# One part of the input split a chunk sooner, a fourth low part by DMA, and another order of buffers in the last way down

## The chip, the cores and the metric

The kernel is one launch on one core of a Trainium2 chip. The metric is the device time of a launch in microseconds, the median of several runs; lower is better. The core has five engines that each work through a queue of their own in order and meet only at semaphores: TensorE (PE, matmuls and weight loads), VectorE (DVE), ScalarE (ACT), GpSimd (POOL) and SyncE (SP, which here issues nearly all loads). PE accumulates into banks of PSUM, 128 x 512 floats each.

## The reference

A trunk of two layers over 512 tokens of width 1024. Each layer is a half-step SwiGLU FFN, a mixer (mLSTM in layer 0, gMLP in layer 1), a second FFN and a gated per-layer embedding ("ple"), each added to `x` and normalised. The change lies in the FFNs, of which there are four:

```python
def swiglu_ffn(x, w_gu, w_d):                 # x 512 x 1024, w_gu 1024 x 5632, w_d 2816 x 1024
    g, u = jnp.split(x @ w_gu, 2, axis=-1)
    return (jax.nn.silu(g) * u) @ w_d
# in each layer i:
x = layer_norm(ALPHA * x + 0.5 * swiglu_ffn(x, ffn1_wgu[i], ffn1_wd[i]), ...)
x = layer_norm(ALPHA * x + mixer(x), ...)
x = layer_norm(ALPHA * x + 0.5 * swiglu_ffn(x, ffn2_wgu[i], ffn2_wd[i]), ...)
x = layer_norm(ALPHA * x + sigmoid(x @ ple_wg[i] + ple_bg[i]) * (p[i] @ ple_wp[i]), ...)
```

Everything is float32.

## The kernel before

**High and low parts.** A float32 operand is taken apart into a high part in the type float32r (`whi`, `xh`, `fhi`) and what is left, the low part (`wlo`, `xl`, `flo`). A product of two operands is three matmuls, high x high, high x low and low x high: `mm3`, lines 353 to 355. The high part is a copy by ACT. The low part is made in one of two ways, in `Weights.fill`:

```python
self.nc.scalar.activation(hi[:, s], src[:, s], AF.Copy)                       # L242
if make in self.by_dma or low == "dma" and make not in self.in_place:
    self.nc.scalar.activation(lo[:, s], src[:, s], AF.Copy, scale=-1.0)       # L248
    self.nc.gpsimd.dma_start(lo[:, s], src[:, s], accum_op=OP.add)            # L249
elif not self.apart:
    self.nc.vector.tensor_sub(lo[:, s], src[:, s], hi[:, s].bitcast(F32))     # L251
```

So a low is a subtraction on DVE, or a second ACT copy with the sign turned and a DMA issued by POOL that adds the source to it ("by DMA"). With `apart`, DVE's subtraction is put off and issued later by `lows()` (L257).

**An FFN in six chunks.** The 22 blocks of hidden columns go in chunks of 2, 4, 4, 4, 4 and 4 (0 to 5). Of each chunk PE computes the way up (gate and up columns), then SiLU x up gives `h`, and `h` goes the way down. The way down of a chunk runs one chunk later, woven into the next way up, in a 2 x 2 block form with 7 products in place of 8 (`Group`; the sums of its weights are formed on DVE in lines 111 to 117, its operand is split in lines 905 and 908, and line 727 adds the product to `x`). The way down of chunk 5 has no way up behind it: it is the "plain" way down, `dps`, with four weight tiles of 128 x 1024 from two loads.

**The way up of chunks 4 and 5** uses 7 products too, per pair of hidden blocks: four pairs in an FFN, 0 and 1 in chunk 4, 2 and 3 in chunk 5. The weights of a pair are two loads (gate and up, 128 x 2048 each) and come in seven forms, `Weights.up_forms`: a11, a12, s2, s1, s3, s4, a22, the products 0 to 6. a11, a12, s4 and a22 are the loaded quarters or what the sums left there; s2 is formed in place on DVE (lines 141, 142), s3 in lines 149 and 150 once the lows of a12 and s2 are made, and s1 is what line 141 left. `UP_BY_DMA` names the products whose low goes by DMA: a12, s3, s4, a22 so far; the lows of a11, s2 and s1 are DVE's.

The other side of these products are forms of `x`: three quarters of `x`, which exist in `xh` and `xl`, and four sums that `UpForms` makes: t3 = x22 - x12, t2 = t3 + x11, t1 = x22 - t2 and t4 = x21 - t2, each of 128 x 1024 and split in a high and a low. The sums take one step at a time of `self.steps` in chunk 3; what `self.last` holds is done in chunk 4 behind the product with that number. Working buffers `b` and `c` carry t3 and t2, `d` carries t4. `c` has the buffer `f0` that t4's low takes over; `b` has the buffer `wlo` of the pool `late` that t2's low takes over, so that t2's low cannot be made before t3 is split from `b`.

A product's turn in `up_products` sets the order of all that the engines get:

```python
pair.product(r)          # PE: 24 matmuls of 128 x 256
group.add()              # DVE: L727 for the product of the way down before
pair.take(r)             # ACT copies the bank to `us` (L1047) for r = 0, 2, 3; DVE adds (L1050) for 1, 4, 5
group.finish_form(); W.lows()                 # DVE: L908, L257
if c == UP_FROM and s in formed.last:
    formed.last[s]()
W.release(); pair.gate(r)                     # more whi/wlo; ACT: Silu (L1061) for r = 1, 5
```

and behind every second product one of the way down. Line 1066 is the multiplication by SiLU, lines 358 and 359 are `split`, line 1000 is t4's high, line 1004 t2's low (t3's split stands in front of it) and line 1009 t4's low.

**Buffers.** Split weights lie in four buffers of kind `main`, which are filled in the order of use as they come free; the forms of the way down lie in a buffer of kind `rows`, and late in pair 3 a second one, `rowsx`, is opened behind product 2 in place of `UpForms`' tiles of the pool `late`. `add_rows` gives the four tiles of the plain way down a kind each. SP issues a load as soon as a raw buffer is free; no queue is ordered by a planner.

Of the kernel before, what the change touches and what calls it, by code (L numbers as in the profile page):

```python
# [10 lines left out]
F32 = mybir.dt.float32  # L11
F32R = mybir.dt.float32r
AF = mybir.ActivationFunctionType
# [29 lines left out]
W_BUFS = 4  # L43
EXTRA = 2
PLE_EXTRA = 3
UP_BY_DMA = (1, 4, 5, 6)


class Weights:
# [77 lines left out]
    def up_forms(self, g, u):  # L127
# [34 lines left out]
        self.after.update({s2: (a11,), s3: (a12, s2)})  # L162
        self.by_dma.update(made[r][1] for r in UP_BY_DMA)
        return [("main", js, make) for js, make in made]
# [158 lines left out]
def hybrid_trunk(ctx: ExitStack, tc, x, p, ln_g, ln_b, ffn1_wgu, ffn1_wd, ffn2_wgu, ffn2_wd,  # L323
# [25 lines left out]
    vec, sca, pool = nc.vector, nc.scalar, nc.gpsimd  # L349
# [7 lines left out]
    def split(hi, lo, src):  # L357
        sca.activation(hi, src, AF.Copy)
        vec.tensor_sub(lo, src, hi.bitcast(F32))
# [51 lines left out]
    def kp(w):  # L411
        return w.rearrange("(kb p) c -> p kb c", p=P)
# [4 lines left out]
    def add_pairs(w, a0, b0):  # L417

        W.add((w_cols(w, a0), cols2), (w_cols(w, b0), cols2))

    def kinds_of(kind, at):
        return kind if isinstance(kind, str) else kind[at:at + 2]

    def add_rows(w, kb, n, kind="main"):
        for k in range(0, n, 2):
            W.add((kp(w)[:, kb + k:kb + k + 2, :], rows2), kind=kinds_of(kind, k))
# [9 lines left out]
    LAST = len(FFN_CHUNKS) - 1  # L436
# [4 lines left out]
    def ffn_weights(wgu, wd, name, ple=False):  # L441
        starts = [sum(FFN_CHUNKS[:c]) for c in range(LAST + 1)]

        def forms(c):
            m = FFN_CHUNKS[c] // 2

            def quarter(i, j):
                k = starts[c] + m * i
                return kp(wd)[:, k:k + m, j * 512:(j + 1) * 512]
            loads = [W.add_load(quarter(i, j), n, name) for i, j, n in ((0, 0, 2), (0, 1, 1), (1, 1, 1), (1, 0, 2))]  # L450
            return W.forms("rows", *((j, slice(None)) for j in loads))

        first = len(W.order)
        for at in range(starts[UP_FROM]):
            if at == 0 or at == starts[UP_FROM] - 1:
                W.add(*((kp(wgu)[:, :, c0:c0 + P], [slice(None)]) for c0 in (at * P, HID + at * P)))
            elif at % 2:
                add_pairs(wgu, at * P, HID + at * P)
        tiles = W.order[first:]
        del W.order[first:]  # L460
        for c, n in enumerate(FFN_CHUNKS):
            down_w = deque(forms(c - 1) if c else ())
            if c >= UP_FROM:
                products = []
                for b in range(starts[c], starts[c] + n, 2):
                    products += W.up_forms(*(W.add_load(kp(wgu)[:, :, c0:c0 + 2 * P], 2) for c0 in (b * P, HID + b * P)))
                for s, product in enumerate(products):
                    W.order.append(product)
                    if s % 2:
                        W.order.append(down_w.popleft())  # L470
                continue
            for i in range(2 * n):
                W.order.append(tiles[2 * starts[c] + i])
                if down_w:
                    W.order.append(down_w.popleft())
        if ple:
            W.add_hook("rows", lambda hi, lo: turn_p.pop()(hi, lo))
        add_rows(wd, starts[LAST], 4, ["rows", "rowsx", "main", "main"] if ple else ["main", "rows", "rows", "rowsx"])


    ML_SLOTS = (2, 3, 4, 5, 6, 7, 11)
# [71 lines left out]
    def ple_weights(i):  # L553
        add_rows(ple_wp[i], 0, 2)
        add_wide(ple_wg[i], 0, ["extra", "extra", "extra", "main"])
        add_wide(ple_wg[i], 512, ["rows", "rows", "rowsx", "rows2"])

    ffn_weights(ffn1_wgu[0], ffn1_wd[0], (0, 0))
    ml_weights()
    ffn_weights(ffn2_wgu[0], ffn2_wd[0], (0, 2), True)  # L560
    ple_weights(0)
    ffn_weights(ffn1_wgu[1], ffn1_wd[1], (1, 0))
    gm_weights()
    ffn_weights(ffn2_wgu[1], ffn2_wd[1], (1, 2), True)
# [108 lines left out]
    class Norm:  # L673


        def __init__(self, layer, k, out=None):
            self.out, self.st, self.rs = out, {}, {}
            self.deferred = out is None and k != 2
            self.at = (layer * 4 + k) * KB
            gb = act.tile([P, 2, D], F32, name="gb", tag="gb")  # L680
            self.g_bc, self.b_bc = gb[:, 0], gb[:, 1]
            o = (layer * 4 + k) * D
            sca.dma_start(self.g_bc, row_ap(ln_g, o, D))
            sca.dma_start(self.b_bc, row_ap(ln_b, o, D))
# [265 lines left out]
    class UpForms:  # L950


        def __init__(self, pool, late):

            f32 = lambda at, tag: at.tile([P, 4, 256], F32, name="x_" + tag, tag=tag)
            a = [tmp.tile([P, 2, 256], F32, name="x_a", tag="pad", bufs=3) for _ in range(2)]
            b, c = f32(late, "wlo"), f32(pool, "f0")
            both = act.tile([P, 2, 4, 256], F32R, name="t1", tag="gb")
            self.t1, self.t2, self.t4 = [both[:, 0], both[:, 1]], [], []
            self.t3 = self.quarter(0, 1)  # L960
            whole, halves = slice(0, 4), (slice(0, 2), slice(2, 4))

            def joined(dst, k, t, s=whole):
                vec.tensor_add(dst, *(p[:, s].bitcast(F32) for p in self.quarter(k, t)))

            def f32r(to, at, tag):
                to.append(at.tile([P, 4, 256], F32R, name="t_" + tag, tag=tag))
                return to[-1]

            def x22():  # L970
                for i, s in enumerate(halves):
                    joined(a[i], 1, 1, s)

            def t3():
                for i, s in enumerate(halves):
                    vec.tensor_sub(b[:, s], a[i], b[:, s])

            def t1():
                for i, s in enumerate(halves):
                    vec.tensor_sub(a[i], a[i], c[:, s])  # L980

            def split_t1():
                for i, s in enumerate(halves):
                    split(self.t1[0][:, s], self.t1[1][:, s], a[i])

            self.steps = [
                x22, lambda: joined(b, 0, 1), t3, lambda: joined(c, 0, 0), lambda: vec.tensor_add(c, b, c),
                lambda: sca.activation(f32r(self.t2, late, "whi"), c, AF.Copy), t1, split_t1]

            d = [tmp.tile([P, 2, 256], F32, name="x_d", tag="pad", bufs=3) for _ in range(2)]  # L990

            def x21():
                for i, s in enumerate(halves):
                    joined(d[i], 1, 0, s)

            def t4():
                hi = f32r(self.t4, pool, "f1")
                for i, s in enumerate(halves):
                    vec.tensor_sub(d[i], d[i], c[:, s])
                    sca.activation(hi[:, s], d[i], AF.Copy)  # L1000

            def t3_t2():
                split(*self.t3, b)
                vec.tensor_sub(f32r(self.t2, late, "wlo"), c, self.t2[0].bitcast(F32))

            def t4_low():
                lo = f32r(self.t4, pool, "f0")
                for i, s in enumerate(halves):
                    vec.tensor_sub(lo[:, s], d[i], self.t4[0][:, s].bitcast(F32))

            self.steps += [x21, t4]
            self.last = {0: t3_t2, 3: t4_low}
            self.right = [self.quarter(0, 0), self.quarter(1, 0), self.t2, self.t1, self.t3,
                          self.quarter(1, 1), self.t4]

# [894 lines left out]
```

## Time and profile before

| | |
|---|---|
| median of 3 runs | 2246.17 us (2243.39 to 2249.09) |
| the profiled execution | 2251.26 us, its span 2249.5 |
| mean granted TensorE clock in the span | 0.994 |
| packets of DMA | 287.31 MB, of these POOL's queue 58.91 MB |
| copies to `whi` from 128 x 1024 or smaller tiles of `wraw` on ACT (L242) | 388, 1047 ns each |
| matmuls of the way up in 7 products (`ups`, three lines) | 3 x 512, 285 to 288 ns each |

How to read it: a group has its line, engine, operation, tiles and shapes, then busy time and mean length of one, then the idle time of the engine just ahead of these instructions and what ended it. In the lists of single instructions the first number is the start in us from the begin of the span, the second the length (with "x2" and more: of all of them together, gaps included). The granted clock is the share of full speed that TensorE was allowed.

### The profile page before, as it was taken

The page shows a single profiled execution, that of the slowest core. Times are in us where ns is not written, and L with a number is a line of the kernel's source. Part 1 is how long each engine was busy: PE and PEld are TensorE (multiplying, and loading weights), DVE is VectorE, ACT ScalarE, POOL GpSimd, SP SyncE. Part 2 cuts the span into 40 slices and gives each one's busy share as a digit, 9 for nine tenths or more (in the row PEclk, how much of TensorE's full clock was granted, in tenths as well). Part 3 has the DMA queues.
Part 4 walks back from the last instruction along what each step waited for, and adds up shares of the span by engine and source line. Part 5 has one row for each costly group of instructions (what it writes and reads, how often), then busy time and mean ns, then how long its engine had stood idle before and what let it go on. Part 6 is the DMA issues. An engine that isn't in the chain of part 4 may idle for free. (4 is left out here: it accounts for less than half of the span.)

```text
span 2249.5 us, 29438 instructions
## 1 busy us (share of the span) xinstructions
PE 2207.3 (98%) x11669; PEld 1896.6 (84%) x11669; DVE 1693.8 (75%) x2452; ACT 1059.5 (47%) x1492; POOL 159.0 (7%) x199
## 2 busy tenths in 40 slices
PE   9999999999999999999999999999999999999998
PEld 8888987888888888888888888987888888888877
DVE  5668787786776776688786768886788767678887
ACT  4334655464646433356444334655345453336542
POOL 1000110111101100001000000110001100001000
PEclk9999999999999999999999999999999999999999
DMA  6323754456847443246532333754437733335551
GB/s 200 104 93 113 179 137 131 108 143 133 155 123 155 126 131 94 93 121 161 169 122 66 115 101 112 178 135 137 140 76 151 168 122 113 103 113 124 139 168 57
DMA packets 215538, 287.31 MB, mean 128 GB/s; under 512 B 6836, under 2 KB 161588, under 8 KB 215400
## 3 DMA queue, kind: packets, MB, share of 16 engines
q1 hardware_dynamic: 168080, 211.83, 29.2%
q0 software_dynamic: 40704, 58.91, 16.4%
q10 hardware_dynamic: 6616, 14.69, 2.0%
q8 instruction: 92, 1.51, 0.3%
q14 instruction: 46, 0.38, 0.1%
HBM read 224.58 MB, written 2.11 MB: 101 GB/s over the span
## 5 line engine op out<-in xcount | busy, mean ns | idle before, releaser
L242 ACT ACTIVATE whi<-wraw 128x1024 fp32r<-128x1024 f32 (+1 forms) x388 | 400.0, 1047 | 247.8 <-DVE wraw L142 90.8
L353 PE MATMUL fps<-xh,whi 128*128 128x512 f32 x800 | 311.4, 389 | 0.0
L354 PE MATMUL fps<-xl,whi 128*128 128x512 f32 x800 | 311.2, 389 | 0.0
L355 PE MATMUL fps<-xh,wlo 128*128 128x512 f32 x800 | 311.2, 389 | 0.0
L251 DVE TENSOR_TENSOR wlo<-wraw,whi 128x1024 fp32r<-128x1024 f32 (+1 forms) x214 | 257.0, 1216 | 52.5 <-ACT whi L242 51.9
L353 PE MATMUL gps<-whi,fhi 128*128 128x512 f32 x644 | 251.9, 391 | 0.0
L354 PE MATMUL gps<-wlo,fhi 128*128 128x512 f32 x644 | 251.6, 391 | 0.0
L355 PE MATMUL gps<-whi,flo 128*128 128x512 f32 x644 | 251.3, 390 | 0.0
L242 ACT ACTIVATE whi<-wquarter 128x1024 fp32r<-128x1024 f32 (+1 forms) x140 | 135.6, 969 | 201.0 <-PE gps L355 132.8
L249 POOL DMA_DIRECT2D wlo<-wraw x112 | 114.2, 1020 | 1500.5 <-ACT wlo L248 1309.6
L251 DVE TENSOR_TENSOR wlo<-wquarter,whi 128x1024 fp32r<-128x1024 f32 (+1 forms) x92 | 97.6, 1061 | 160.6 <-ACT whi L242 160.6
L727 DVE TENSOR_TENSOR xt<-xt,gps 128x512 f32<-128x512 f32 x302 | 193.0, 680 | 1.2 <-PE gps L355 1.2
L355 PEld LDWEIGHTS fps<-xh,wlo 128*128 128x128 f32 x800 | 150.2, 188 | 31.3
L353 PEld LDWEIGHTS fps<-xh,whi 128*128 128x128 f32 x800 | 150.2, 188 | 31.1
L354 PEld LDWEIGHTS fps<-xl,whi 128*128 128x128 f32 x800 | 150.2, 188 | 30.9
L353 PE MATMUL ups<-xh,whi 128*128 128x256 f32 x512 | 147.6, 288 | 12.2 <-ACT us L1047 12.2
L355 PE MATMUL ups<-xh,wlo 128*128 128x256 f32 x512 | 147.5, 288 | 1.1 <-DMA wlo<-wraw 1.1
L354 PE MATMUL ups<-xl,whi 128*128 128x256 f32 x512 | 146.1, 285 | 0.0
L355 PEld LDWEIGHTS gps<-whi,flo 128*128 128x128 f32 x644 | 120.9, 188 | 26.2
L353 PEld LDWEIGHTS gps<-whi,fhi 128*128 128x128 f32 x644 | 121.1, 188 | 23.9
L354 PEld LDWEIGHTS gps<-wlo,fhi 128*128 128x128 f32 x644 | 121.1, 188 | 23.6
L905 ACT ACTIVATE fhi<-h 128x512 fp32r<-128x512 f32 (+1 forms) x140 | 80.8, 577 | 120.2 <-DVE h L1151 50.4
(361 smaller groups left out, 5056.5 us busy)
## 6 DMA issues: line engine op xcount, KB each, us to landing
wraw<-in_ffn_wgu_dram SPq DMA_DIRECT2D x79, 1024.0 KB, 7.3
wlo<-wraw POOLq DMA_DIRECT2D x112, 512.0 KB, 5.9
wquarter<-in_ffn_wd_dram SPq DMA_DIRECT2D x64, 512.0 KB, 3.8
wraw<-in_ml_w_in_dram SPq DMA_DIRECT2D x24, 1024.0 KB, 5.8
wraw<-in_gm_w_in_dram SPq DMA_DIRECT2D x15, 1024.0 KB, 5.6
wraw<-in_ffn_wgu_dram SPq DMA_DIRECT2D x17, 512.0 KB, 4.9
wraw<-in_ffn_wd_dram SPq DMA_DIRECT2D x8, 1024.0 KB, 6.3
wraw<-in_ml_w_out_dram SPq DMA_DIRECT2D x8, 1024.0 KB, 5.1
```

The lines of the kernel that those rows point to most:

```text
L242: self.nc.scalar.activation(hi[:, s], src[:, s], AF.Copy)
L249: self.nc.gpsimd.dma_start(lo[:, s], src[:, s], accum_op=OP.add)
L251: self.nc.vector.tensor_sub(lo[:, s], src[:, s], hi[:, s].bitcast(F32))
L353: mm(ps, st[0], mv[0], start=start, stop=False, skip_group_check=more)
L354: mm(ps, st[0], mv[1], start=False, stop=False, skip_group_check=more)
L355: mm(ps, st[1], mv[0], start=False, stop=stop, skip_group_check=more)
L727: vec.tensor_add(dst, dst, ps)
L905: sca.activation(hi, src, AF.Copy)
```

## The change

It has three parts, and each applies to all four FFNs.

1. t2 gets its low in chunk 3, behind its high, by `split`; for that `b` moves to the buffer `f1`, which t4's high takes over. t4's high in turn moves from chunk 3 to chunk 4, behind product 3, and t4's low from behind product 3 to behind product 4 of the first pair.
2. s1's low goes by DMA.
3. The four weight tiles of the plain way down take other buffers: where the ple follows (FFNs 1 and 3) `rowsx` and `rows` change places, and in FFNs 0 and 2 `rowsx` holds the third tile and `rows` the second and fourth.

```diff
-UP_BY_DMA = (1, 4, 5, 6)
+UP_BY_DMA = (1, 3, 4, 5, 6)
...
-        add_rows(wd, starts[LAST], 4, ["rows", "rowsx", "main", "main"] if ple else ["main", "rows", "rows", "rowsx"])
+        add_rows(wd, starts[LAST], 4, ["rowsx", "rows", "main", "main"] if ple else ["main", "rows", "rowsx", "rows"])
...
-            b, c = f32(late, "wlo"), f32(pool, "f0")
+            b, c = f32(pool, "f1"), f32(pool, "f0")
...
+            def split_t2():
+                split(f32r(self.t2, late, "whi"), f32r(self.t2, late, "wlo"), c)
+
             self.steps = [
                 x22, lambda: joined(b, 0, 1), t3, lambda: joined(c, 0, 0), lambda: vec.tensor_add(c, b, c),
-                lambda: sca.activation(f32r(self.t2, late, "whi"), c, AF.Copy), t1, split_t1]
+                split_t2, t1, split_t1]
...
             def t4():
+                for i, s in enumerate(halves):
+                    vec.tensor_sub(d[i], d[i], c[:, s])
+
+            def t4_high():
                 hi = f32r(self.t4, pool, "f1")
                 for i, s in enumerate(halves):
-                    vec.tensor_sub(d[i], d[i], c[:, s])
                     sca.activation(hi[:, s], d[i], AF.Copy)
-
-            def t3_t2():
-                split(*self.t3, b)
-                vec.tensor_sub(f32r(self.t2, late, "wlo"), c, self.t2[0].bitcast(F32))
...
-            self.last = {0: t3_t2, 3: t4_low}
+            self.last = {0: lambda: split(*self.t3, b), 3: t4_high, 4: t4_low}
```

SP's order of loads is the same in both; POOL's queue gets four more DMAs in each FFN. From the second hunk on, line numbers are higher by 2 or 3 in the new kernel (L1047 is L1049, L1050 is L1052, L1061 is L1063, L1151 is L1153).

How it moves instructions, at three places. A row is line, operation, output <- inputs and shape, in the order of the engine's queue; "x2" stands for two in a row.

DVE in FFN 0, around the first product of chunk 4, before (`x_f_1300` is the buffer `c`, `x_wlo` the buffer `b`; the row of L1004 is t2's low, the first L251 the low of s1):

```order
L1151 SCALAR_TENSOR_TENSOR h<-sg,fps 128x512
L251 TENSOR_TENSOR wlo<-wraw,whi 128x1024
L251 TENSOR_TENSOR wlo<-wquarter,whi 128x1024
L908 TENSOR_TENSOR flo<-h,fhi 128x512
L359 TENSOR_TENSOR xl<-x_wlo,xh 128x4x256
L1004 TENSOR_TENSOR t_wlo<-x_f_1300,t_whi 128x1024
L149 TENSOR_TENSOR wraw<-wraw 128x1024
L150 TENSOR_TENSOR wraw<-wraw 128x1024
```

and now (`x_f_1299` is the buffer `b`):

```order
L1153 SCALAR_TENSOR_TENSOR h<-sg,fps 128x512
L251 TENSOR_TENSOR wlo<-wquarter,whi 128x1024
L908 TENSOR_TENSOR flo<-h,fhi 128x512
L359 TENSOR_TENSOR xl<-x_f_1299,xh 128x4x256
L149 TENSOR_TENSOR wraw<-wraw 128x1024
L150 TENSOR_TENSOR wraw<-wraw 128x1024
```

Two subtractions fewer stand ahead of L149 and L150. t2's low stands about seventeen rows earlier in this queue, behind the step that makes t2 in chunk 3.

ACT at the same place, before (the row of L1000 is t4's high in two halves, the first L242 the high of s2, the second that of s1, the row of L1047 the copy behind product 0):

```order
L242 ACTIVATE whi<-wraw 128x1024
L1000 ACTIVATE t_f_1710<-x_d 128x512 x2
L905 ACTIVATE fhi<-h 128x512
L242 ACTIVATE whi<-wraw 128x1024
L242 ACTIVATE whi<-wquarter 128x1024
L905 ACTIVATE fhi<-h 128x512
L1047 ACTIVATE us<-ups 128x512
```

and now (the row of L248 is s1's copy with the sign turned, for the DMA):

```order
L242 ACTIVATE whi<-wraw 128x1024
L905 ACTIVATE fhi<-h 128x512
L242 ACTIVATE whi<-wraw 128x1024
L248 ACTIVATE wlo<-wraw 128x1024
L242 ACTIVATE whi<-wquarter 128x1024
L905 ACTIVATE fhi<-h 128x512
L1049 ACTIVATE us<-ups 128x512
```

t4's high is gone from here, and s1's second copy stands two rows further on.

DVE in pair 2 of FFN 0, from the low of s2 to the addition for the gate, before (the second `wlo<-wraw` is s1's low):

```order
L257 TENSOR_TENSOR wlo<-wraw,whi 128x1024
L149 TENSOR_TENSOR wraw<-wraw 128x1024
L150 TENSOR_TENSOR wraw<-wraw 128x1024
L257 TENSOR_TENSOR wlo<-wraw,whi 128x1024
L257 TENSOR_TENSOR wlo<-wquarter,whi 128x1024
L908 TENSOR_TENSOR flo<-h,fhi 128x512
L727 TENSOR_TENSOR xt<-xt,gps 128x512 x2
L111 TENSOR_TENSOR wquarter<-wquarter 128x1024
L112 TENSOR_TENSOR wquarter<-wquarter 128x1024
L1050 TENSOR_TENSOR us<-us,ups 128x512
```

and now:

```order
L257 TENSOR_TENSOR wlo<-wraw,whi 128x1024
L149 TENSOR_TENSOR wraw<-wraw 128x1024
L150 TENSOR_TENSOR wraw<-wraw 128x1024
L257 TENSOR_TENSOR wlo<-wquarter,whi 128x1024
L908 TENSOR_TENSOR flo<-h,fhi 128x512
L727 TENSOR_TENSOR xt<-xt,gps 128x512 x2
L111 TENSOR_TENSOR wquarter<-wquarter 128x1024
L112 TENSOR_TENSOR wquarter<-wquarter 128x1024
L1052 TENSOR_TENSOR us<-us,ups 128x512
```

One subtraction fewer stands between L150 and the addition.

ACT at the end of FFN 0's last pair, before (the rows of L242 here are the highs of the plain way down's tiles and, behind them, of the mixer's weights; `gb` are the layer norm's weights):

```order
L1047 ACTIVATE us<-ups 128x512
L242 ACTIVATE whi<-wraw 128x1024 x2
L683 DMA gb<-in_ln_g_dram 128x1024
L684 DMA gb<-in_ln_b_dram 128x1024
L1061 ACTIVATE us<-us 128x512
L358 ACTIVATE wquarter<-us 128x2x256 x2
L242 ACTIVATE whi<-wraw 128x1024 x5
```

and now:

```order
L1049 ACTIVATE us<-ups 128x512
L242 ACTIVATE whi<-wraw 128x1024 x3
L683 DMA gb<-in_ln_g_dram 128x1024
L684 DMA gb<-in_ln_b_dram 128x1024
L1063 ACTIVATE us<-us 128x512
L358 ACTIVATE wquarter<-us 128x2x256 x2
L242 ACTIVATE whi<-wraw 128x1024 x4
```

The high of the third tile has moved ahead of the two loads and of the Silu in line 1061, now 1063.

## The prediction

> **What bounds the kernel now.** I read the page first, then the waits of PE, then the places of those waits in order of time.
>
> ```profile
> span 2249.5 us, 29438 instructions
> PE 2207.3 (98%) x11669; PEld 1896.6 (84%) x11669; DVE 1693.8 (75%) x2452; ACT 1059.5 (47%) x1492; POOL 159.0 (7%) x199
> ```
>
> PE is busy for 98% of the span and the change leaves its matmuls as they are. So it can only touch the idle 42 us and the matmuls that run at a lower clock. The waits of PE, longest in total first (line waited for: total us, times, longest):
>
> ```profile
> PE ups L353 <- ACT us L1047: 12.2, 12, 2.5
> PE dps L353 <- DVE xt L727: 7.0, 3, 3.5
> PE ups L354 <- DVE t_wlo L1004: 5.1, 4, 1.3
> PE dps L353 <- ACT whi L242: 2.4, 2, 1.2
> PE ups L355 <- DMA wlo<-wraw: 2.2, 3, 1.1
> PE dps L354 <- DVE wlo L257: 1.5, 2, 0.8
> ```
>
> That is 30.4 us. All of it lies in the last two chunks of the four FFNs and the plain way down behind them, which is where the change works. I number the FFNs 0 to 3 and the pairs of an FFN's last two chunks 0 to 3.
>
> **Part one: t2 is split a chunk sooner.** Pair 0 of FFN 0, start and length of each row, idle time before it in brackets:
>
> ```profile
> 222.81 0.38 PE L354 MATMUL ups<-t_wlo,whi 128*128 128x256 f32 x1 [1.29 <-DVE t_wlo L1004]
> 221.53 1.23 DVE L1004 TENSOR_TENSOR t_wlo<-x_f,t_whi 128x1024 fp32r<-128x1024 f32 x1
> 223.92 1.22 DVE L150 TENSOR_TENSOR wraw<-wraw 128x1024 f32<-128x1024 f32 x1
> 213.21 1.24 ACT L1000 ACTIVATE t_f<-x_d 128x512 fp32r<-128x512 f32 x2 [3.10 <-DVE x_d L999]
> 225.18 1.06 ACT L242 ACTIVATE whi<-wraw 128x1024 fp32r<-128x1024 f32 x1 [5.53 <-DVE wraw L150]
> 240.60 0.28 PE L354 MATMUL ups<-t_f,whi 128*128 128x256 f32 x1
> 201.54 1.23 DVE L251 TENSOR_TENSOR wlo<-wquarter,whi 128x1024 fp32r<-128x1024 f32 x1 [2.18 <-ACT whi L242]
> ```
>
> Removed: PE stands still for just the 1.29 us of t2's low; four times, the 5.1 of the waits. Of the 12.2 us for the copies `us`, 7.0 stand in pair 2 (below) and 4.4 in pair 3; the other 0.8, 0.2 in each FFN, stand right behind this wait and hang on L150, which comes earlier, so they go too. Added a chunk sooner: DVE waits for t2's high (one ACT copy, 1.06) and makes the low (1.23). I cost this 2.3 us at nothing, because DVE stood idle for 2.18 us at 201.54; 0.2 us would remain if the cover failed, more only if it were gone.
>
> Moved: t4's high goes from chunk 3 to product 3 and its low behind product 4's lows. DVE has no gap from L150 on except for about 0.5 us twice, where it waits for ACT. Ahead of L150 its queue loses t2's low and s1's low, and the 1.24 us of t4's high no longer stand ahead of the fhi copy that DVE waits for; going through the queue with these durations, L150 starts at about 221 (2.9 sooner) and t4's low has its first half at 239.6. PE, 1.5 us sooner, wants it at 240.60 - 1.5 = 239.1. That is a new wait of 0.5 us, between 0 and 2.0 (if DVE gained only 1.2 us). Four times: +2.0. Part one: -5.1 - 0.8 + 2.0 = **-3.9**.
>
> **Part two: s1's low by DMA.** It moves 16 lows (4 FFNs x 4 pairs) from DVE to ACT and POOL; each costs by these groups:
>
> ```profile
> L248 ACT ACTIVATE wlo<-wraw 128x1024 fp32r<-128x1024 f32 x112 | 116.9, 1044 | 0.0
> L257 DVE TENSOR_TENSOR wlo<-wraw,whi 128x1024 fp32r<-128x1024 f32 x62 | 74.4, 1219 | 6.1 <-ACT whi L242 6.0
> ```
>
> So DVE has 16 x 1.219 = 19.5 us less, ACT 16 x 1.044 = 16.7 us more. What of this reaches PE is decided in pair 2, where the long waits stand (DVE, ACT and PE of FFN 0, then the same PE wait of the other FFNs):
>
> ```profile
> 273.74 1.23 DVE L141 TENSOR_TENSOR wraw<-wraw 128x1024 f32<-128x1024 f32 x1 [6.84 <-DMA wraw<-in_ffn_wgu_dram]
> 284.58 1.22 DVE L257 TENSOR_TENSOR wlo<-wraw,whi 128x1024 fp32r<-128x1024 f32 x1
> 279.11 1.04 ACT L242 ACTIVATE whi<-wraw 128x1024 fp32r<-128x1024 f32 x1
> 284.75 1.06 ACT L242 ACTIVATE whi<-wraw 128x1024 fp32r<-128x1024 f32 x1 [2.65 <-DVE wraw L150]
> 291.75 0.63 ACT L1061 ACTIVATE us<-us 128x512 f32<-128x512 f32 x1 [3.09 <-DVE us L1050]
> 286.27 0.28 PE L353 MATMUL ups<-t,whi 128*128 128x256 f32 x1
> 294.38 0.39 PE L353 MATMUL ups<-xh,whi 128*128 128x256 f32 x1 [2.37 <-ACT us L1047]
> 1059.49 0.38 PE L353 MATMUL ups<-xh,whi 128*128 128x256 f32 x1 [1.62 <-ACT us L1047]
> 1475.16 0.39 PE L353 MATMUL ups<-xh,whi 128*128 128x256 f32 x1 [0.54 <-ACT us L1047]
> 2109.84 0.39 PE L353 MATMUL ups<-xh,whi 128*128 128x256 f32 x1 [2.49 <-ACT us L1047]
> ```
>
> Product 4 waits for the copy `us`, which stands in ACT's queue behind the Silu of 291.75, which waits for DVE's L1050. The row at 284.58 is s1's low; without it everything behind it on DVE comes 1.14 us sooner. The start of the chain, L141, waits for a load that is issued when a low of pair 1 has landed; that low hangs on pair 1's L150, about 2.4 us sooner. So the chain is some 2.4 + 1.1 = 3.5 us ahead, PE itself 1.5 - 0.5 = 1.0: the waits shrink by up to 2.5. All four go: 2.37 + 1.62 + 0.54 + 2.49 = 7.0 (4.7 if the start moves by 1.3 only; 0 if ACT's new copies took it back). For the same reason the three waits for a low by DMA (2.2) go, and FFN 2's 0.6 in pair 3. Together **-9.8**. The other 3.8 us of pair 3 (0.5, 1.8 and 1.5 in FFNs 0, 1 and 3) are bound by ACT's own queue, without a gap from L150's copy to `us`, and stay.
>
> ACT's copies of 1.04 us are hidden: in pair 0 they take the place of t4's high, in the others they fall into the idle time ahead of the next copy (the 2.65 us at 284.75). In pair 3 of FFNs 1 and 3 one puts product 2 off by about 0.4 us, which the wait behind takes up.
>
> The landing is the unknown: from issue to landing took these DMAs in pair 2, late in pair 0 with two loads of weights beside one, and in the median of FFN 0:
>
> ```profile
> wlo<-wraw POOLq DMA_DIRECT2D x2, 512.0 KB, 5.0
> wlo<-wraw POOLq DMA_DIRECT2D x1, 512.0 KB, 9.2
> wlo<-wraw POOLq DMA_DIRECT2D x16, 512.0 KB, 5.4
> ```
>
> In pair 2 s1's high ends at 280.15, the second copy at 281.1, the DMA is issued 0.3 later and lands at 286.4; 2.4 us sooner that is 284.0. PE wants it with the third matmul after 286.27, at 286.5 - 1.0 = 285.5. So 1.5 us are left; with 9.2 us it is 2.7 late. The row nearest to it is pair 2's own, 5.0, so most of the 16 wait for nothing, and for a few beside a load I take +1.5 together (bounds 0 and 16 x 2.7 = 43).
>
> **Part three: the buffers of the last way down.** FFN 1 (as FFN 3), then FFN 0, then the second load of FFN 2's weights:
>
> ```profile
> 1107.36 2.95 ACT L242 ACTIVATE whi<-wraw 128x1024 fp32r<-128x1024 f32 x3 [0.94 <-PE gps L355]
> 1108.46 0.50 PE L353 MATMUL dps<-whi,wquarter 128*128 128x512 f32 x1 [1.19 <-ACT whi L242]
> 1108.44 6.90 DVE L257 TENSOR_TENSOR wlo<-wraw,whi 128x1024 fp32r<-128x1024 f32 x6 [1.30 <-ACT whi L242]
> 1115.26 1.27 DVE L727 TENSOR_TENSOR xt<-xt,gps 128x512 f32<-128x512 f32 x2
> 345.49 1.06 ACT L242 ACTIVATE whi<-wraw 128x1024 fp32r<-128x1024 f32 x1 [1.09 <-DMA wraw<-in_ml_w_in_dram]
> wraw<-in_ffn_wd_dram SPq DMA_DIRECT2D x1, 1024.0 KB, 8.5
> ```
>
> In FFNs 1 and 3 the first tile can only be split when the last group product is done (the wait of 1.19, and 0.76 for its low). In `rowsx` it is split before; the second tile then waits 0.65. The way down's second block still needs L727, which stands behind the six lows: one less is 1.15 sooner. So -1.15 in FFN 1; in FFN 3 PE does not wait for L727 (the 7.0 us have three entries, FFNs 0 to 2), so 1.95 - 0.65 = -1.3. In FFN 0 the wait of 3.5 for L727 ends with the load of 345.49, which does not move: 0. In FFN 2 the third tile's high now waits on ACT, ahead of the Silu, for a load of 8.5 us: between 0 and +1.8, I take +0.6 because the layer norm's loads then come behind it. **-1.85**.
>
> **Part four: the clock.** Stretches of 3.41 us, PE busy first, granted clock behind the engines:
>
> ```profile
> 292.48:295.89 3.41, 1.51 (x12) 1.51 (x13) 3.41 (x5) 3.41 (x5) 0.00 (x0) 1.00 0.48 86
> 295.89:299.30 3.41, 3.41 (x18) 3.41 (x17) 3.38 (x5) 2.57 (x4) 0.85 (x1) 0.50 1.06 330
> 1057.07:1060.48 3.41, 1.79 (x12) 1.33 (x11) 3.38 (x6) 3.41 (x6) 0.00 (x0) 1.00 0.54 101
> 1060.48:1063.89 3.41, 3.41 (x30) 3.41 (x30) 3.38 (x4) 2.58 (x4) 0.84 (x1) 1.00 0.98 311
> ```
>
> After a stretch in which PE was busy for 1.51 us the clock is 0.50 for a whole stretch; after one with 1.79 it is not. At half clock 1.7 us are lost, and without the wait of 2.37 that goes: **-1.7**. The Trainium skill (TensorE: Matmul & The Clock Gate, What's actually happening) has a window of 3413 ns that runs freely, which these rows agree with, and the half clock after an idle window; taken as a wholly idle one, no wait here would bring it, this term would be 0, and the sum -14.1. The row with 1.51 us of work says otherwise.
>
> Sum: -3.9 - 9.8 + 1.5 - 1.85 - 1.7 = -15.8. The profiled execution took 2251.3, its span 2249.5; it would be 2235.5. The median of the three runs is 5 us below it, so I predict 2246.2 - 15.8 = 2230.
>
> **Rivals.** *Slower: s1's low comes late.* For it speaks the row of 9.2 us. The Trainium skill (DMA: Bandwidth & Descriptors, Queues, rings and completion order) has every DMA engine go round the queues that hold work, so that a low beside a load would take about twice as long; the two landings agree. Were product 3 late by half of pair 2's 2.7 in the mean, it would cost 16 x 1.35 = 21.6: -17.3 + 21.6 = +4, 2250. It decides from 17.3 / 16 = 1.1 us of lateness on, which is a landing of 5.0 + 1.5 + 1.1 = 7.6 us in the mean. Against it stands the median of 5.4 in FFN 0. *ACT takes back what DVE gains:* the copies delay `us` as much as DVE frees it. Then parts one and three are left, -5.8, 2240. Against it stand ACT's gaps of 2.65 and 5.53 us ahead of L150's copy. *More goes:* t4's low is in time (-2.0), and a second half-clock stretch vanishes (-1.7) with the late lows (-1.5): 2225.
>
> **Chances.** Forecast 0.56, more goes 0.18, ACT takes it back 0.19, late low 0.07. Of the third about two thirds fall within 0.3% (6.7 us, about what a measurement of this kernel can tell from no change), of the last half is slower. So faster 0.81, same 0.15, slower 0.04. The range, 2224 to 2241, leaves out the late low and a little on the other side.
>
> **What would show it.** Right: no `t_wlo` among PE's waits; `us` there at about 4 us instead of 12.2; L1050 and the Silu in pair 2 some 3.5 us ahead; `dps` no longer waiting for `whi`; a clock of 0.997. A small wait of `ups` L354 for t4's low would show the price of part one. Wrong: a total for `ups` L355 on DMA well over 2.2 us (late lows), `us` still near 10 us (ACT), or the Silu before FFN 2's way down waiting for its load.

## The result and the profile after

The change takes the median from 2246.19 us (2243.39 to 2249.09) to 2231.63 us (2227.36 to 2233.93): a ratio of 0.9931, 95% interval 0.9918 to 0.9945, or 14.6 us less. Predicted were 2230 and -15.8. Of all the executions in this document one is out of line, of part three alone: it took 11637 us, and counts in that kernel's median below, not in its ratio or clock. The profiled execution of the changed kernel took 2233.93 us, with this head of the page:

```profile
span 2232.2 us, 29495 instructions
PE 2198.6 (98%) x11669; PEld 1890.0 (85%) x11669; DVE 1675.1 (75%) x2436; ACT 1073.7 (48%) x1508; POOL 172.7 (8%) x215
```

PE's idle time, span less busy time, went from 42.2 to 33.6 us, and its busy time for the same 11669 matmuls from 2207.3 to 2198.6. The latter is mostly the clock: PE worked for 18.7 us at half clock before and for 3.1 us now, and half of that is lost (by this estimate 9.4 and 1.6 us). The waits of PE (line waited for: total us, times, longest):

```profile
PE dps L353 <- DVE xt L727: 8.1, 4, 3.5
PE ups L353 <- ACT us L1049: 5.4, 7, 1.3
PE ups L354 <- DVE t_f L1011: 3.2, 4, 0.8
PE ups L355 <- DMA wlo<-wraw: 2.7, 4, 0.9
PE dps L354 <- DVE wlo L257: 1.9, 3, 0.8
PE gps L353 <- ACT fhi L905: 0.9, 1, 0.9
```

t2's low (5.1) and the `whi` of the plain way down (2.4) are gone, `us` has shrunk from 12.2, and a new wait for t4's low (L1011) has come. Pair 0 of FFN 0, as in the prediction:

```profile
221.40 1.23 DVE L150 TENSOR_TENSOR wraw<-wraw 128x1024 f32<-128x1024 f32 x1
237.98 1.22 DVE L257 TENSOR_TENSOR wlo<-wquarter,whi 128x1024 fp32r<-128x1024 f32 x1
239.11 1.28 DVE L1011 TENSOR_TENSOR t_f<-x_d,t_f 128x512 fp32r<-128x512 f32 x2
239.85 0.39 PE L354 MATMUL ups<-t_f,whi 128*128 128x256 f32 x1 [0.81 <-DVE t_f L1011]
```

L150 started at 221.4, predicted about 221; t4's low stands behind two lows of weights (the second at 237.98), and PE waits 0.81 us for its first half, predicted 0.5. Pair 2 of FFN 0 now has no wait for `us`. There the Silu starts here:

```profile
286.31 0.63 ACT L1063 ACTIVATE us<-us 128x512 f32<-128x512 f32 x1 [1.96 <-DVE us L1052]
```

That was 291.75 before; PE itself began this pair at 273.81 instead of 274.90, so the Silu is 4.4 us earlier against PE (predicted: 3.5, less 1.0). That is the best of the four: counted from the pair's first matmul, the Silu of pair 2 came 0.3 and 2.7 us sooner in FFNs 2 and 3 and 2.1 us later in FFN 1, in the mean 1.3 us sooner (1.2 in the repeat below). FFN 1 shows what did not go as planned, pair 2's first load and what came of it:

```profile
wraw<-in_ffn_wgu_dram SPq DMA_DIRECT2D x1, 1024.0 KB, 10.6
1033.38 1.23 DVE L141 TENSOR_TENSOR wraw<-wraw 128x1024 f32<-128x1024 f32 x1 [10.35 <-DMA wraw<-in_ffn_wgu_dram]
1038.89 0.50 PE L353 MATMUL gps<-whi,fhi 128*128 128x512 f32 x1 [0.92 <-ACT fhi L905]
1052.89 0.39 PE L353 MATMUL ups<-xh,whi 128*128 128x256 f32 x1 [0.86 <-ACT us L1049]
```

The load, issued at 1022.68, landed after 10.6 us; the same load of before took 8.0 us, 5.4 in its repeat. So DVE stood still for 10.35 us ahead of L141, and the chain of this pair starts late whatever stands in DVE's queue.

### The profile page after: what moved, and what is told of

Same layout as the page of the kernel before. It is cut to its first block, busy times and chain, and to the rows that moved or that the text cites. A ratio compares the mean times of both kernels' runs of the same rounds, so it can differ in the third digit from the quotient of the medians.

```text
span 2232.2 us, 29495 instructions
## 1 busy us (share of the span) xinstructions
PE 2198.6 (98%) x11669; PEld 1890.0 (85%) x11669; DVE 1675.1 (75%) x2436; ACT 1073.7 (48%) x1508; POOL 172.7 (8%) x215
## 3 DMA queue, kind: packets, MB, share of 16 engines
q0 software_dynamic: 43008, 67.30, 18.7%
q8 instruction: 92, 1.51, 0.3%
## 5 line engine op out<-in xcount | busy, mean ns | idle before, releaser
L242 ACT ACTIVATE whi<-wraw 128x1024 fp32r<-128x1024 f32 (+1 forms) x388 | 400.7, 1047 | 243.9 <-DVE wraw L142 63.7
L251 DVE TENSOR_TENSOR wlo<-wraw,whi 128x1024 fp32r<-128x1024 f32 (+1 forms) x210 | 252.1, 1215 | 53.2 <-ACT whi L242 52.4
L249 POOL DMA_DIRECT2D wlo<-wraw x128 | 127.8, 999 | 1474.7 <-ACT wlo L248 1219.6
L242 ACT ACTIVATE whi<-wquarter 128x1024 fp32r<-128x1024 f32 (+1 forms) x140 | 135.6, 968 | 200.8 <-PE gps L355 132.5
L251 DVE TENSOR_TENSOR wlo<-wquarter,whi 128x1024 fp32r<-128x1024 f32 (+1 forms) x92 | 97.6, 1061 | 151.9 <-ACT whi L242 151.9
L727 DVE TENSOR_TENSOR xt<-xt,gps 128x512 f32<-128x512 f32 x302 | 193.0, 680 | 1.2 <-PE gps L355 1.2
L908 DVE TENSOR_TENSOR flo<-h,fhi 128x512 fp32r<-128x512 f32 (+1 forms) x140 | 88.8, 635 | 67.4 <-ACT fhi L905 66.6
```

Source lines behind the costliest of these rows:

```text
L727: vec.tensor_add(dst, dst, ps)
```

## The experiments

Each was timed beside the kernel before. "Clock" is the mean over a kernel's timed runs.

| kernel | median us | ratio to before, interval | clock |
|---|---|---|---|
| before, once more | 2247.47 | 0.9996, 0.9988 to 1.0005 | 0.9960 |
| part one alone | 2240.86 | 0.9965, 0.9953 to 0.9977 | 0.9955 |
| part two alone | 2242.47 | 0.9971, 0.9960 to 0.9983 | 0.9960 |
| part three alone | 2244.88 | 0.9989, 0.9980 to 0.9998 | 0.9962 |
| changed, once more | 2233.73 | 0.9943, 0.9931 to 0.9956 | 0.9970 |
| changed without part two | 2236.78 | 0.9955, 0.9939 to 0.9972 | 0.9968 |
| changed, t4's low sooner | 2229.29 | 0.9923, 0.9909 to 0.9936 | 0.9978 |
| changed, PE kept busy | 2227.36 | 0.9912, 0.9898 to 0.9925 | 0.9988 |
| changed, addition first | 2222.03 | 0.9889, 0.9874 to 0.9904 | 0.9990 |
| both edits | 2221.83 | 0.9889, 0.9866 to 0.9911 | 0.9985 |
| both, a22's low on DVE in chunk 5 | 2222.92 | 0.9893, 0.9869 to 0.9918 | 0.9990 |

Theory: the gain is the sum of PE's waits that go, plus the half-clock stretches that hung on them. Rivals: one part makes all of it; the parts share one gain; the clock's part is luck of two profiles.

**Before, once more.** No edit.

> The kernel of before once more, unchanged, to see what a repeat shows: time 0 +- 1 us. The profile of before had five half-clock stretches inside the span (six of 3.41 us), each behind a long wait of PE; the full change had one. If a stretch belongs to a place, the same places show it again and the clock is 0.994. If it is where a free-running window of 3.41 us happens to fall on a wait, the places differ, the number is anything from 2 to 6 and the granted clock varies from run to run, with it the time: about 1.7 us per stretch, which is the size of the spread between runs of the same kernel.

The half-clock stretches lay elsewhere in part: in the first profile of before at 295.89, 347.09 (two), 1091.2, 1528.1 and 2159.57, now at 348.49 (two), 1526.09, 2109.77 and 2157.55. Three places are the same, the waits for L727 in FFNs 0 and 2 and the start of FFN 3's last way down; the stretches of FFN 0's pair 2 and FFN 1's pair 3 did not come again, and one came in FFN 3's pair 2. Stretches of 3.41 us behind a wait of PE in two places, and the stretch after each (PE busy first, granted clock behind POOL):

```profile
290.46:293.87 3.41, 1.70 (x8) 1.05 (x6) 3.38 (x5) 1.72 (x3) 0.00 (x0) 1.00 1.03 195
293.87:297.28 3.41, 2.50 (x21) 2.50 (x22) 3.41 (x5) 3.41 (x6) 0.36 (x1) 1.00 0.44 121
2106.35:2109.77 3.42, 1.19 (x10) 1.19 (x11) 3.38 (x6) 3.42 (x6) 0.00 (x0) 1.00 0.52 96
2109.77:2113.18 3.41, 3.41 (x19) 3.41 (x18) 3.38 (x5) 2.58 (x4) 0.86 (x1) 0.50 1.00 325
```

FFN 0's pair 2 waited as long as before (2.62 us) and this time had no stretch, because the wait lay on a window's border and left 1.70 us of work in one window and 2.50 in the next. FFN 3's pair 2 (a wait of 2.59) fell into one window and had one. So a stretch belongs to a wait and to where the window falls, not to a place alone. The Trainium skill (TensorE: Matmul & The Clock Gate, What's actually happening) calls the window free-running and the number of slow matmuls at a kernel's start different from run to run; these rows agree, and show the same in the middle of a kernel. Its table, though, has the half clock follow an idle window, and PE worked for 1.19 us in the one that starts at 2106.35: the measurement decides. There is no sharp limit in what the records show as busy. In all thirteen profiles of this case, windows at full clock with up to 1.51 us of work brought it each time, of those with 1.56 to 1.76 some did (1.64 and 1.75 in the first profile) and some not (1.64 and 1.70 in the repeat), and none above. The fastest and the slowest runs fit: in 54 runs of the kernel before, those with a clock of 0.995 took 2248.3 us in the mean (17 runs), those with 0.997 2245.4 (14).

**Part one alone.** `UP_BY_DMA` and the buffers as before.

> Part one alone (t2 split in chunk 3, t4 a few products later), s1's low still on DVE, old buffers. My theory (the gain is PE's waits, summed, and half-clock stretches that hang on them): the four waits of 1.29 us for t2's low and the four of 0.2 us behind them go (-5.9), but s1's low still stands in DVE's queue ahead of L150, so t4's low is later than in the full change, where PE waited 0.81 us for it: I expect 0.8 to 2.0 us in each FFN, say 1.2, +4.8. Sum -1 us (range -3 to +2). The waits for the copies us in pairs 2 and 3 stay at about 11 us and the clock stays near 0.994 to 0.995. Rival (each part's gain is its own): t4's low waits 0.81 as in the full change, and the part is worth -2.7 with nothing else moved.

Wrong: 6 us less, where I expected about 1 and at most 3. The wait for t4's low came as expected, 1.40 us in each FFN (the last line is L150 of pair 0 in FFN 0):

```profile
PE dps L353 <- DVE xt L727: 8.4, 3, 4.5
PE ups L353 <- ACT us L1049: 8.2, 7, 2.1
PE ups L354 <- DVE t_f L1011: 5.6, 4, 1.4
221.61 1.23 DVE L150 TENSOR_TENSOR wraw<-wraw 128x1024 f32<-128x1024 f32 x1
```

But `us` fell from 12.2 (12.6 in the repeat) to 8.2. t2's low was 1.2 us of work in the stretch where DVE has no gap, and moving it to chunk 3, where it has some, lets all of chunk 4's queue and the loads behind it start sooner: L150 of pair 0 starts 8.69 us after the pair's first matmul instead of 11.18, and in pair 2 of FFN 0 6.87 instead of 8.54 (in the mean of the four FFNs' pairs 2, where loads of different lengths come in, 7.0 instead of 7.9). I had counted that gain for part two. PE's idle time is 38.4 us, 3 to 4 less than before, and the mean clock of the runs is no better than before; where the rest of the 6 us lies these figures do not show.

**Part two alone.**

> Part two alone (s1's low by DMA), t2's low still in chunk 4, old buffers. My theory: pair 2's 7.0 us for us shrink to about 1.5 as in the full change (-5.5); t2's low loses the 1.2 us of s1's low ahead of it on DVE, so its waits of 1.29 us shrink to about 0.2 (-4.4); no new wait for t4; late lows +0.5. Half-clock stretch behind pair 2 of FFN 0 goes, -1.7, that of pair 3 of FFN 1 perhaps too. Sum about -11.5 (range -8 to -15), that is most of the change. Rival (ACT takes back what DVE gains): us stays near 10 us and the time near before. Rival (late low): ups L355 on DMA well over 5 us and the time above before.

Wrong: less than half of what I expected, and outside the range. `us` did fall, to 6.5, but t2's low was still waited for 0.8 us in each FFN, since DVE now waited for ACT ahead of it (L150 only 0.5 us sooner), and lows by DMA came late:

```profile
PE ups L353 <- ACT us L1047: 6.5, 10, 1.3
PE ups L355 <- DMA wlo<-wraw: 5.4, 6, 2.0
PE ups L354 <- DVE t_wlo L1004: 3.2, 4, 0.8
1483.40 0.39 PE L355 MATMUL ups<-t_f,wlo 128*128 128x256 f32 x1 [2.04 <-DMA wlo<-wraw]
```

The longest was not s1's low but a22's, the last product's (`t_f` is t4).

**Part three alone.**

> Part three alone (the buffers of the last way down). My theory: the two waits of 1.19 us for whi in FFNs 1 and 3 go, FFN 1 is about 1.0 better, FFN 3 only 0.2 (a wait for L727 of 1.0 takes the place), FFNs 0 and 2 unchanged: -1 to -1.5, and -1.7 more if the half-clock stretch in FFN 3 hung on that wait: -2.5. All other waits as before. Rival: nothing at all, 0 +- 1, because the wait only moves from the first tile to the banks.

As expected: 2.4 us less by medians. In FFN 3 the two waits of 1.19 and 0.76 became 0.76 and 0.98, the second one for L727, which had no wait there before.

**Changed, once more, and without part two.**

> The changed kernel once more, unchanged: 2231.5 +- 1.5 us, some 15 us below the kernel before. By the free-running window of 3.41 us, half-clock stretches come only behind waits that take over half of a window, and few waits here are long enough: FFN 0's wait of 3.5 us for L727 always, FFN 2's of 2.6 in some runs. So one or two stretches inside the span, mean granted clock of the runs 0.997 to 0.998 against 0.9956 of the kernel before. Rival: if the changed kernel's one stretch was luck of that profile, the mean clock of its runs comes out near that of before.

The repeat gives the same within the interval. Its profile has two stretches while PE works, behind FFN 0's and FFN 2's waits for L727. Over its nine runs the mean clock is 0.9973, over 54 of before 0.9959. A thousandth of mean clock is 0.002 x 2240 = 4.5 us at half speed, so 2.2 us lost: the clock is worth 1.4 x 2.2 = 3 us. PE's busy time in the two profiles of each (2207.3 and 2206.9 against 2198.6 and 2200.5) would make it 7.5, but those are two draws.

> The changed kernel without part two: s1's low on DVE again, parts one and three as they are. Part two alone took about 5 us off the kernel before, and the three parts alone add up to the whole (7.1 + 5.1 + 2.3 against 14.6); so taking it out here should cost 5 to 6 us: 2238 (range 2235 to 2241), with t4's low waited for 1.4 us in each FFN as in part one alone, us at about 8 us, and a clock near 0.996. Rival (the parts share one gain, since each shortens the same queue): it costs 2 us or less.

It costs 3 us against the repeat's median, 4 by the means (2236.8 against 2232.7 over nine runs of the changed kernel), where part two alone had taken 5: so by the medians part two has a gain of its own beside the other parts. The two intervals overlap, though, and the profile does not show the gain:

```profile
PE ups L354 <- DVE t_f L1011: 5.6, 4, 1.4
PE ups L353 <- ACT us L1049: 5.4, 4, 2.0
```

t4's low was waited for as expected, but `us` for 5.4 us and not 8, as in the changed kernel, and 2.0 us of that stand in pair 2. PE's idle time is 33.5 us, against 33.6 and 33.8 with part two. So in this profile the waits for `us` in pair 2 go without part two as well; what part two takes away is 2.4 us of t4's waits, and in these profiles late lows, `fhi` and `us` give that back. The medians of the parts alone, 6.4, 4.8 and 2.4 below the kernel before measured beside them, add up to 13.7, and the whole took 14.6 and 12.0 in its two sets.

**t4's low sooner.**

```diff
                     group.finish_form()
-                    W.lows()
                     if c == UP_FROM and s in formed.last:
                         formed.last[s]()
+                    W.lows()
```

> The changed kernel with t4's low put ahead of the two lows of weights (L257) behind product 4, instead of behind them; nothing else. PE waited 0.81 us for it in each FFN. My theory: DVE makes the same work in another order, t4's low ends 2.4 us sooner, the four waits go (-3.2); the pushed lows are of pair 1 and of the next product down and have more than 1.2 us to spare. A part may be given back in pair 2, where the chain hangs on loads: -2 us against the changed kernel (range -3.2 to 0). Rival (DVE is the bound there): the pushed lows are waited for instead, and the time is the same.

The four waits went, and the time fell by 4.4 us against the repeat of the changed kernel, measured beside it, 2.3 against its first runs. Expected were 2 and at most 3.2, so against the repeat it is more than the theory gives. A part is the clock (0.9978 against 0.9970, by the figures above some 1.8 us): in this profile FFN 0's wait of 3.4 us for L727 lay on a window's border, left 1.76 and 1.70 us of work in the two windows and brought no half clock, where I had written "always" of this wait. The wait for DMA was higher (6.0, longest 2.3, and behind that one came the profile's only half-clock stretch while PE works), so the rest of the chain gave some back.

**PE kept busy.** `busy` is set in FFNs 0 and 2 only.

```diff
+            if t == 1 and busy:
+                spare = up_bank("warm")
+                for _ in range(8):
+                    mm(spare, hs[0][0][:, :P], ws[0][0][:, 0, :512], start=True, stop=True)
             banks = [dn_bank("dps"), dn_bank("dps")]
```

> The changed kernel with eight extra matmuls of 512 columns (1.9 us of work whose result nobody reads) on PE ahead of the last way down's second block in FFNs 0 and 2, where PE stands still for 3.5 and 2.6 us. No wait becomes shorter. My theory of the clock (half speed for one window of 3.41 us after a window in which PE was busy for less than about half): FFN 0's window is filled up and its half-clock stretch goes, FFN 2's too where it fell in one; -1.7 to -2.5 us against the changed kernel, with the matmuls added, and the clock 0.998 or 0.999. Rival (the stretch follows from the wait itself, not from PE's work in the window): no change, or up to 1 us slower where the extra work sticks out.

PE got 16 matmuls more and the kernel became 6.4 us faster than the repeat, 4.3 faster than the first runs of the changed kernel. The place in FFN 0, then the window in which the extra matmuls lie and the two behind it:

```profile
339.47 1.98 PE L776 MATMUL warm<-whi,wquarter 128*128 128x512 f32 x8
343.08 0.50 PE L353 MATMUL dps<-whi,wquarter 128*128 128x512 f32 x1 [1.64 <-DVE xt L727]
338.27:341.68 3.41, 3.18 (x15) 2.29 (x13) 1.71 (x3) 1.06 (x1) 0.00 (x0) 1.00 0.98 315
341.68:345.09 3.41, 2.00 (x9) 1.68 (x10) 3.38 (x6) 0.00 (x0) 0.00 (x0) 1.00 0.82 309
345.09:348.50 3.41, 3.41 (x17) 2.83 (x16) 2.62 (x6) 0.00 (x0) 0.57 (x1) 1.00 0.00 0
```

The same place in the changed kernel:

```profile
343.13 0.80 PE L353 MATMUL dps<-whi,wquarter 128*128 128x512 f32 x1 [3.55 <-DVE xt L727]
339.43:342.84 3.41, 0.15 (x1) 0.00 (x0) 1.68 (x3) 1.06 (x1) 0.00 (x0) 1.00 1.04 396
342.84:346.25 3.41, 3.12 (x7) 2.48 (x8) 3.34 (x6) 0.00 (x0) 0.00 (x0) 0.50 0.47 174
```

The block starts when L727 lets it, 343.08 as against 343.13, with full clock after it where the changed kernel has 0.50 from 342.84 on. The windows lie otherwise here, so the rows are not the same stretch twice: the 1.98 us of extra matmuls all fall into the window from 338.27, which would have had 1.20 us of work without them, and up to 1.51 us brought half clock each time. The 2.00 us in the next window are the way down's own matmuls. So the half clock does hang on PE's work in the window, and not on the moment at which the block can start. The clock of 0.9988 against 0.9973 accounts for 3.3 us. The rest, 1 to 3 us, does not come from the extra matmuls as far as the runs show: in this profile `us` was waited for 2.2 us, against 5.4 and 6.4, and FFN 1's first load of pair 2 landed after 5.8 us.

**Addition first.** The last L727, which frees the PSUM banks, ahead of the pending lows:

```diff
+                if h is None:
+                    W.lows(3 if prepare is not None else 0)
+                    group.add()
                 W.lows()
```

> The changed kernel with the last product's addition to x (L727), which frees the PSUM banks, issued ahead of the pending lows at the end of the way up (behind three of them in FFNs 1 and 3), instead of behind all. The changed kernel waits there 3.5, 0.95, 2.6 and 0.98 us in FFNs 0 to 3 (8.1 in all). My theory: these waits go but for some 0.3 us in the first block, where the last tile's low is now 1.2 us later: -7.5, and with FFN 0's wait its half-clock stretch: -1.7. Sum -9 us against the changed kernel (range -6 to -11), clock 0.998. Rival: the lows that are pushed back belong to the mixer's and the ple's weights and are waited for there: then -2 or less.

11.7 us less than the repeat of the changed kernel, a little more than the range, and 9.6 less than its first runs; no wait of PE for L727 is left, and no half-clock stretch while PE works. DVE in FFN 0 in the changed kernel (first line) and now, and PE's waits now:

```profile
342.39 1.28 DVE L727 TENSOR_TENSOR xt<-xt,gps 128x512 f32<-128x512 f32 x2
335.94 1.28 DVE L727 TENSOR_TENSOR xt<-xt,gps 128x512 f32<-128x512 f32 x2
337.13 3.49 DVE L257 TENSOR_TENSOR wlo<-wraw,whi 128x1024 fp32r<-128x1024 f32 x3
PE ups L355 <- DMA wlo<-wraw: 3.8, 2, 2.2
PE ups L353 <- ACT us L1049: 3.5, 5, 1.2
PE ups L354 <- DVE t_f L1011: 3.2, 4, 0.8
PE dps L354 <- DVE wlo L257: 2.8, 3, 1.3
```

L727 comes at 335.94 instead of 342.39. PE's idle time fell from 33.6 to 25.4 us, and the clock (0.9990 against 0.9973) is worth some 3.7 us more. In FFN 2 the first block waits 1.3 us for a low that was pushed back, the price.

**Both edits, and a22's low.** `both` joins the two; in the second, `up_forms` gets `by_dma=UP_BY_DMA[:-1] if c == LAST else UP_BY_DMA`.

> The changed kernel with both edits, t4's low ahead of the two lows and the last product's addition ahead of the pending ones. By the waits of their own profiles they lie in different places (pair 0; the last way down), so they add up: add_first less 3 us, about 2219 (range 2217 to 2222), 27 us below the kernel before. Rival: a PE that comes 0.8 us sooner to pair 2 waits there for a22's low by DMA (2.2 us in add_first's FFN 2) or for us; then it is add_first's time.

> Kernel both with a22's low back on DVE in chunk 5 (pairs 2 and 3); chunk 4 as it was. In add_first PE waited 2.2 us in FFN 2 and 1.6 in FFN 1 for a22's low by DMA, which is issued in the same moment as a load of 1 MB and lands after 9.0 us. If the late low by DMA is a real cost of that step, these waits go (-3.8 in such a profile) and 8 subtractions of 1.22 us come back on DVE, ahead of pair 3's L141: I expect 1 to 3 us less than both. Rival (DVE's time is worth more than the landing): pair 3's waits for us grow by 1.2 us each and the time is the same or up to 3 us more.

For `both` the rival holds: no difference from the addition alone (2221.83 and 2222.03), though the median also lies at the upper end of the range that I gave. t4's waits are gone, and a22's low in pair 2 is waited for instead. The issue of the low and of the load that goes out in the same moment (SP's and POOL's, in the kernel with the addition first), then the wait in `both`:

```profile
wraw<-in_ffn_wgu_dram SPq DMA_DIRECT2D x1, 1024.0 KB, 7.0
wlo<-wraw POOLq DMA_DIRECT2D x1, 512.0 KB, 9.0
1469.82 0.39 PE L355 MATMUL ups<-t_f,wlo 128*128 128x256 f32 x1 [2.60 <-DMA wlo<-wraw]
PE ups L355 <- DMA wlo<-wraw: 6.7, 6, 2.6
```

The wait of 2.60 us and one of 1.94 in FFN 0 each brought a half-clock stretch in this profile. With a22's low on DVE the waits for DMA fall to 0.7, and `us` (whose copy is L1050 in this kernel) rises to 9.2 from 3.7:

```profile
PE ups L353 <- ACT us L1050: 9.2, 8, 1.5
PE ups L355 <- DMA wlo<-wraw: 0.7, 2, 0.5
```

Here the rival holds again: 6 us of one wait are exchanged for 5.5 of the other, at the same time (2222.92). They do not lie in the same place: 5.7 of the 6.7 us for the lows stand in pair 2, and 8.8 of the 9.2 us stand in pair 3, as the rival has it.

## Why the prediction came out

The time was right, and so was the kind of mechanism, waits of PE that go and half-clock stretches that go with them. But the largest term was over-sized and is not shown to belong to the part that it was given to, the clock's was under-sized, and that the two errors hid each other is luck. The measured waits are those of the profiles of the changed kernel, with its repeat behind a slash.

- **t2's low, -5.9:** right. All four waits and the 0.2 us behind each are gone.
- **t4's low, +2.0:** a wait at the place named, 3.2 / 3.2. The queue was followed rightly up to L150; 0.3 us per FFN were missing at its end.
- **`us`, DMA and FFN 2's pair 3, -9.8 with +1.5 for late lows:** over-sized. `us` fell by 6.8 / 5.8 (of this 0.8 is counted above), the DMA's waits came to 2.7 / 1.7 against 2.2 before, and a new wait of 0.9 / 1.5 for `fhi` stands in FFN 1: some -4.3 in place of -8.3. The step that failed is "all four go": pair 2's waits fell from 7.0 to 1.6 / 1.7, and 1.4 of that stands in FFN 1 both times. The start of pair 2's chain is a load, and where that landed after 10.6 us, DVE's gain did not reach the chain. FFN 2's 0.6 in pair 3, which was to go too, became 1.3 / 2.3. And the gain in pair 2 is not shown to be part two's: without part two its waits were 2.0, and part one alone took `us` down by 4.
- **Buffers, -1.85:** about -1.2 (`whi` 2.4 less, L727 and the low together 1.5 / 0.9 more). "In FFN 3 PE does not wait for L727" failed: its wait of 0.98 was hidden behind the two that went.
- **Clock, -1.7:** under-sized, since I counted one stretch as if it had a place. Each wait over half a window is a draw; fewer of them make fewer stretches everywhere. About -3 by the runs' clocks, up to -8.7 in the two profiles that I compared.

In the two profiles the waits gave 8.6 where I had 14.1, and PE's shorter busy time the other 8.7. Those are two executions: with the clock of the runs, 8.6 and 3 make some 12 of the 14.6 us, and the rest is not placed. The rival of late lows is true in a form of its own: a22's low, not s1's, lands late in pair 2, up to 2.3 us in the changed kernel with t4's low sooner and 2.6 in `both`, and s1's product waited only once in each profile of the changed kernel, for 0.31 us. How the waits in pairs 2 and 3 are shared out differs by 2 us from one execution to the next, so a single pair of profiles does not settle the terms finer than that, and why FFN 1's load took 10.6 us, and 11.0 in the repeat, is open; in the kernel with the addition first it took 8.1, and with PE kept busy 5.8.

## What to carry to other kernels

When a subtraction is moved out of a stretch where an engine has no gap, price the whole queue behind it and the loads that hang on it, not only the wait that it ends. Before an operand is split sooner, look at what else stands in the queue ahead of the work that frees banks or buffers: here one call moved past the pending lows was worth 10 to 12 us, the whole change 12 to 15. And once PE waits for little, the waits for two paths (a subtraction on DVE, a low by DMA) are exchanged for one another: look at whether a path has room before work is moved onto it.

## What the runs showed of the hardware

Half clock came for a whole window of 3.41 us after every window in which PE had worked for up to 1.51 us, after some with 1.56 to 1.76 us and after none at full clock with 1.79 us or more. 16 useless matmuls in two waits kept the clock up (0.9988 in the mean of the runs, against 0.9973), and the kernel with them was 4 to 6 us faster, of which the clock accounts for 3.3. The same kernel had some of its stretches in other places in the next execution, while within an execution the windows' borders keep one grid: from 295.89 to 347.09 are 15 times 3.413. And a window at half clock with 2.05 us of work (347.09; 2.69 at 348.49 in the repeat) was followed by a second one at half clock, so that FFN 0's wait cost two; behind those with 3.0 us and more the clock was full again.
